# Where tiles lie in the on-chip memory: streamed tiles 64 bytes behind their weights modulo 256, in a two-network fp32 kernel on one Trainium2 core

## The chip, the core and the metric

The kernel runs on one core of a Trainium2 chip. TensorE multiplies, VectorE (DVE) and ScalarE (ACT) do the elementwise work, SyncE (SP) issues the loads, and GpSimd (POOL) has next to nothing to do. The metric is the time on the device in microseconds; a lower one is better. The kernel's median over 3 runs is 2473.17 us (2472.64 to 2473.49).

## The reference

Two networks of two layers each, one after the other, on 256 tokens of 1024 features, all in fp32. Each layer of the first network (block 1) has modulated norms, windowed and grouped-query attention over the tokens and 256 context tokens, two up-projections weighted by gates, and a gated feed-forward. Each layer of the second has a feed-forward, a mixer of three attentions (forgetting, stick-breaking, and one with selected keys), and a second feed-forward. Cut to the products that fill TensorE:

```python
def swiglu_2(h, w_gu, w_down):
    g, u = jnp.split(h @ w_gu, 2, axis=-1)
    return (jax.nn.silu(g) * u) @ w_down

# block 1, per layer
h = modulate(rms_norm(x, norm1[l]), sh1, sc1)
na_q, na_k, na_v, gq, gk, gv, ga, gb = jnp.split(h @ w_in[l], IN_SPLITS, axis=-1)
...
x = x + g1 * branch_merge(ya, yb, ga, gb, w_pa[l], w_pb[l], w_o[l])
h2 = modulate(rms_norm(x, norm2[l]), sh2, sc2)
x = x + g2 * swiglu(h2, w_ffn_in[l], w_ffn_out[l])
# second network, per layer: feed-forward, mixer, feed-forward
(q_a, k_a, v_a, f_a, q_b, ...) = jnp.split(h @ w_in, _split_points(), axis=-1)
```

## The kernel before

Activations are kept transposed: 128 features on the partitions, tokens along the row, and a k-tile is one such block of 128 features. Every fp32 operand of a large product is split into a high and a low half of type float32r. ScalarE writes the high half (`hi`, line 403), VectorE the rest (`lo`, line 408). A product is then three matmuls per weight block: high weights with the high stream, high weights with the low stream, low weights with the high stream (`group`). All are issued on line 427. In the profile's names the streamed tile stands first and the weights second: `mm<-gh,hwf` streams gh against weights hwf. hwb and lwb are weight halves of block 1, hwf and lwf those of the second network's feed-forwards, hwmx and lwmx those of its mixers.

Streams: hh and hl are block 1's inputs (512 columns for tokens and context in layer 0, 256 columns for tokens in layer 1, where keys still need 512); gh and gl the second network's inputs; acth and actl the gated inner activations on their way down; yh, yl, ybh, ybl, mh, ml the outputs of attention and their gated sums. In the value projections the roles are exchanged: the weight tile streams, and hh or gh stands as weights.

Memory comes from pools that are laid out as two stacks, one from the left (low addresses) and one from the right. On the left lie, in this order, the constants `cp`, the weights `wp` (raw tiles, then eight high and eight low tiles of 512 floats), the small tiles `sp`, and then whatever a stage opens. A pool's tiles follow each other, each rounded up to 32 bytes, so that the width of one small tile shifts everything behind it. In the built program the weights' halves begin at 39,552 and 55,936, both 128 modulo 256, and step by 2048. The starts of streams modulo 256 are: gh, gl and block 1's mh, ml 224; acth, actl, ybh, ybl, yh, yl and the mixers' mh, ml 0; block 1's hh and hl first 32 and 160 (layer 0's attention, where yh and yl of its merge lie at 32 too), later 0 and 128. hh and hl have rows of 516 floats per k-tile, 2064 bytes; layer 1's feed-forward uses two columns more than 512 (`unnormed` writes columns 512 and 513). Attention's own tiles lie on the right side, at 224.

The order of instructions is made by a scheduler from the program's own order, with a few ties that the kernel adds. `hold` and `queue` make one of them: after the last instruction of a step, a set number (the skip) of later weight splits on VectorE may pass, and the next ten must wait behind it. MIX_HOLD is the skip for a mixer's last normalised input tile (gl at k-tiles 6 and 7).

Of the kernel before, what the change touches and what calls it, by code (L numbers as in the profile page):

```python
# [8 lines left out]
F32 = mybir.dt.float32  # L9
F32R = mybir.dt.float32r  # L10
# [6 lines left out]
P = 128  # L17
DM = 1024
SEQ = 256
NKT = DM // P  # L20
# [112 lines left out]

MIX_HOLD = 5
MIX_ORDER = (
    "K S0 G8 T0 T1 F0 s0 S2 s1 S1 G1 G9 s3 G10 F1 s2 s4 x0 B3 G5 x2 G4 x1 d1 F2 x3 d0 G2 G0 G11 x4 x5 d2 d3 B1 G7 G3 d4 d5 A0 B2".split()
)
# [177 lines left out]

SWAP1 = [p ^ 1 for p in range(32)]
SWAP2 = [p ^ 8 if p < 16 else p for p in range(32)]

# [44 lines left out]
class Builder:  # L367
# [208 lines left out]
            self.hi(hh[:, k : k + 2, c], t)  # L576
            self.last_norm = self.lo(hl[:, k : k + 2, c], t, hh[:, k : k + 2, c])

    def inputs_of(self, pool):

        return [pool.tile([P, NKT, 516], F32R, tag=f"h{c}", name=self.u(f"h{c}")) for c in "hl"]


    def setup_mod(self):
# [11 lines left out]
    def pad_mod(self, pool):  # L596
        nc = self.nc

        self.scp = pool.tile([P, NKT, 32], F32, name="scp")
        nc.vector.memset(self.scp, 0.0)  # L600
        nc.vector.tensor_copy(self.scp[:, :, :2], self.sc)
        self.four = pool.tile([P, 2], F32, name="four")
        nc.vector.tensor_tensor(self.four, self.ident[:, 0:2], self.ident[:, 32:34], ALU.add)
        for j in (64, 96):
            nc.vector.tensor_tensor(self.four, self.four, self.ident[:, j : j + 2], ALU.add)
# [210 lines left out]
    def block1(self, layers, fill):  # L816
        nc = self.nc
        with self.open("y0") as yp:
            y = self.y_tiles(yp, 2 * SEQ)
            self.pad_mod(yp)  # L820
            w = Weights(self, "wb1_0")
            with self.open("h0") as hp:
                h = self.inputs_of(hp)
                with self.open("n0", "right") as np_:
                    self.xs = []
                    self.mod_first(np_, h)
                with self.open("a0", "right") as self.ap_:
                    gates = self.b1_attention(0, w, *h, y, 2 * SEQ, yp)
            self.xs, self.xstack = [], ExitStack()
            for i, (key, stack) in enumerate((("xT", self.ctx), ("ctxT", self.xstack))):  # L830
                x = stack.enter_context(self.open(key, "right")).tile([P, NKT, SEQ], F32, name=f"x{i}")
                nc.sync.dma_start(x, self.ins[key])
                self.xs.append(x)
            md = ExitStack()
            rest = fill(md.enter_context(self.open("mod", "right")))
            mr = ExitStack()
            m = self.b1_merge(0, w, y[0], gates, mr.enter_context(self.open("mr0", "right")), 2 * SEQ)
        with self.open("hn") as hn:
            for l in range(layers):
                T = SEQ if l else 2 * SEQ  # L840
                if l:
                    with self.open("y1") as yp:
                        y = self.y_tiles(yp, T)
                        w = Weights(self, "wb1_1")
                        with self.open("a1", "right") as self.ap_:
                            gates = self.b1_attention(1, w, *h, y, T, yp)
                        mr = ExitStack()
                        m = self.b1_merge(1, w, y[0], gates, mr.enter_context(self.open("mr1", "right")), T)
                self.tc.keep_in_program_order(nc.scalar.preload_act_table_set("silu_and_others"))
                self.amplitude(l, 1, len(self.xs))  # L850
                h = self.inputs_of(hn)
                self.residual(
                    l, w, range(NKT), m, T, 16, hn, lambda i: self.norm_mod(l, 1, i, self.xs[i], h, hn, self.rsb[i]),
                    early=(lambda k: self.unnormed(l, k, h)) if l else None, place="ac"[l],
                )
                mr.close()
                if l:
                    self.room2()
                with self.open(f"f{l}") as fp:
                    if l == 0 and layers > 1:  # L860
                        h2 = []

                        def norm(i):
                            if not h2:
                                h2.extend(self.inputs_of(hn))
                            self.norm_mod(1, 0, i, self.xs[i], h2, hn, self.rsb[i])

                        self.b1_ffn(0, w, h, fp, hn, T, rest, norm)
                        h = h2
                    else:  # L870
                        self.b1_ffn(l, w, h, fp, hn, T, rest, None)
                if l == 0:
                    md.close()
                    if layers > 1:
                        self.xstack.close()
                        self.xs = self.xs[:1]
                assert w.off == w.ap.shape[0] and w.i == len(w.spec)
# [74 lines left out]
    def b1_attention(self, l, w, hh, hl, y, T, yp):  # L952
# [3 lines left out]
        full = lambda k: (hh[:, k, :512], hl[:, k, :512])  # L956
        mine = lambda k: (hh[:, k, :T], hl[:, k, :T])
        nt = T // P
        qg = self.small(1, tag="qg", bufs=1)
        nc.vector.tensor_scalar(qg, self.p(f"qg{l}"), HD**-0.5, None, ALU.mult)  # L960
        bias_tile = lambda: ap.tile([P, 2, SEQ], F32, tag="bias", name=self.u("bias"), bufs=2)
        rot = bias_tile()
# [77 lines left out]
        n = B1_ORDER[l].index("|")  # L1040
# [302 lines left out]
    def mix_attention(self, l, w, hh, hl, xs, rsb, yh, yl, op, gates):  # L1343
# [23 lines left out]
        for b in (b1, b2):  # L1367
            t = self.t2("rq")
            self.rope(pairs(t), pairs(b), twice(cr), twice(sr), SWAP2)
            q = ap.tile([P, 2, 512], F32R, tag="cq", name=self.u("cq"), bufs=2)  # L1370
# [27 lines left out]
        for k in range(0, NKT, 2):  # L1398
# [6 lines left out]
            last = self.lo(hl[:, k : k + 2], pairs(t), hh[:, k : k + 2])  # L1405
        self.hold(1, last, MIX_HOLD)

# [8 lines left out]
        def keys(_):  # L1416
# [21 lines left out]
            kk = self.t2("kk")[:, :SEQ]  # L1438
            self.rope(ki, ki, cos[:64], sin[:64], SWAP2)
            self.halves(kk, ki)  # L1440
            ik.extend(self.parts("ik", kk, SEQ, bufs=1))
            self.rope(kv[64:, SEQ:], kv[64:, SEQ:], cos[64:], sin[64:], SWAP2)
            qs[0] = ap.tile([P, 2, SEQ], F32R, tag="iq", name=self.u("iq"), bufs=1)
# [106 lines left out]
    def dsa_keys(self, l, kv, cos, sin, vs):  # L1550
# [8 lines left out]
        kc, kk = self.t2("kc")[:64, :SEQ], self.t2("kk")[:, :SEQ]  # L1559
        self.rope(kc, kp[:64, :SEQ], cos[:64], sin[:64], SWAP2)  # L1560
        self.halves(kk, kc)
# [196 lines left out]
            self.rsb = [self.rstd_rows(ss)]  # L1758

    def setup2(self):  # L1760
        self.one = self.cp.tile([P, 1], F32, name="one")
        self.nc.vector.memset(self.one, 1.0)

    def store(self, out):
# [71 lines left out]
```

## Time and profile before

| what | value |
|---|---|
| median of 3 runs | 2473.17 us |
| the profiled execution's own time | 2474.45 us |
| its span, first to last instruction | 2472.6 us |
| mean granted clock of TensorE | 0.988 |
| PE busy | 2404.3 us, 97% |
| DVE busy | 1821.5 us, 74% |
| ACT busy | 1357.2 us, 55% |
| DMA | 159 GB/s mean, q1 48.8% of 16 engines |

The profile is one execution. The difference between its time and its span lies outside the first and the last instruction. A busy matmul is counted to its modelled end; in a back-to-back run the next one starts long before that, so the distance from one start to the next is the time that a matmul costs, and the listed duration of some 280 ns is longer than that distance.

### The profile page before, as it was taken

What the parts mean: (1) busy time and instruction counts of PE and PEld (TensorE: products, weight loads), DVE (VectorE), ACT (ScalarE), POOL (GpSimd) and SP (SyncE); (2) the same over time, 40 slices, a digit from 0 to 9 for tenths busy, and PEclk for the clock granted to TensorE, in tenths of its full rate; (3) what the DMA queues carried; (4) which work ended last, traced back from release to release, by engine and by line L of the source; (5) the groups of instructions that cost most, each with busy time, mean ns of one, the idle gap of its engine ahead of it and who ended that gap; (6) DMA issues with size and microseconds to landing.
All of it is one profiled execution on the core that took longest, in us unless ns stands there. A gap on an engine that the chain in (4) does not pass through costs nothing.

```text
span 2472.6 us, 45747 instructions
## 1 busy us (share of the span) xinstructions
PE 2404.3 (97%) x17232; PEld 2243.4 (91%) x17232; DVE 1821.5 (74%) x4115; ACT 1357.2 (55%) x2666; POOL 0.2 (0%) x4
## 2 busy tenths in 40 slices
PE   7999999999999999999999999999999999999997
PEld 4877779888888898999999998999999999899997
DVE  5777667885766888776676688886666669888665
ACT  4566544322223676665555567765555556776553
POOL 0000000000000000000000000000000000000000
PEclk9999999999999999999999999999999999899999
DMA  7221462553653333465555553455555555345553
GB/s 276 85 73 52 160 232 95 171 188 131 218 184 119 129 112 115 146 187 183 184 182 181 182 183 117 138 173 184 177 186 187 178 184 183 106 135 188 180 179 103
DMA packets 112542, 393.45 MB, mean 159 GB/s; under 512 B 12480, under 2 KB 13760, under 8 KB 111808
## 3 DMA queue, kind: packets, MB, share of 16 engines
q1 hardware_dynamic: 112320, 390.52, 48.8%
q8 instruction: 136, 2.23, 0.4%
q14 instruction: 86, 0.70, 0.1%
HBM read 389.42 MB, written 1.05 MB: 158 GB/s over the span
## 4 chain that ended last, share of the span: by engine, by line
PE 91%; DVE 5%; ACT 2%; issue 1%; DMA 1%; SPq 0%; DVEq 0%; ACTq 0%
PE mm L427 82%; PE y L427 2%; PE s L427 1%; PE s L798 1%; PE mm L616 1%; PE y L805 1%; DVE lwmx L408 1%; PE s L751 1%; PE y L486 0%; DMA wm0r<-in_wm_dram 0%; DVE kl L408 0%; ACT pt L775 0%; ACT hwmx L403 0%; PE y L682 0%; DVE ptl L408 0%
## 5 line engine op out<-in xcount | busy, mean ns | idle before, releaser
L427 PE MATMUL mm<-hh,hwb 128*128 128x512 f32 (+2 forms) x1176 | 349.1, 341 | 3.1 <-ACT gt L1027 1.6
L427 PE MATMUL mm<-hl,hwb 128*128 128x512 f32 (+1 forms) x1176 | 350.0, 340 | 0.2 <-DVE hl L408 0.2
L427 PE MATMUL mm<-hh,lwb 128*128 128x512 f32 (+2 forms) x1176 | 346.7, 340 | 0.0
L403 ACT ACTIVATE hwb<-wb_0r 128x512 fp32r<-128x512 f32 (+1 forms) x250 | 149.9, 612 | 261.4 <-PE mm L427 242.4
L427 PE MATMUL mm<-gh,hwf 128*128 128x256 f32 x1344 | 272.1, 283 | 0.0
L427 PE MATMUL mm<-gh,lwf 128*128 128x256 f32 x1344 | 270.7, 282 | 0.0
L427 PE MATMUL mm<-gl,hwf 128*128 128x256 f32 x1344 | 270.6, 282 | 0.0
L408 DVE TENSOR_TENSOR lwf<-wf_1r,hwf 128x512 fp32r<-128x512 f32 (+1 forms) x272 | 183.8, 676 | 110.2 <-ACT hwf L403 103.9
L408 DVE TENSOR_TENSOR lwf<-wf_0r,hwf 128x512 fp32r<-128x512 f32 (+1 forms) x272 | 183.6, 676 | 103.4 <-ACT hwf L403 96.7
L403 ACT ACTIVATE hwf<-wf_1r 128x512 fp32r<-128x512 f32 (+1 forms) x272 | 168.2, 619 | 166.6 <-PE mm L427 153.7
L403 ACT ACTIVATE hwf<-wf_0r 128x512 fp32r<-128x512 f32 (+1 forms) x272 | 168.2, 619 | 165.3 <-PE mm L427 149.4
L427 PEld LDWEIGHTS mm<-hh,hwb 128*128 128x128 f32 x1176 | 203.7, 189 | 30.3 <-ACT gt L1027 2.7
L408 DVE TENSOR_TENSOR lwb<-wb_0r,hwb 128x512 fp32r<-128x512 f32 (+1 forms) x250 | 163.6, 666 | 89.5 <-ACT hwb L403 85.5
L427 PEld LDWEIGHTS mm<-hl,hwb 128*128 128x128 f32 x1176 | 204.5, 189 | 25.8 <-DVE hl L408 0.8
L427 PEld LDWEIGHTS mm<-hh,lwb 128*128 128x128 f32 x1176 | 203.9, 189 | 25.4
L403 ACT ACTIVATE hwb<-wb_1r 128x512 fp32r<-128x512 f32 (+1 forms) x242 | 146.6, 612 | 117.6 <-PE mm L427 107.3
L427 PEld LDWEIGHTS mm<-gh,hwf 128*128 128x128 f32 x1344 | 207.5, 189 | 0.0
L427 PEld LDWEIGHTS mm<-gh,lwf 128*128 128x128 f32 x1344 | 206.7, 188 | 0.0
L408 DVE TENSOR_TENSOR lwb<-wb_1r,hwb 128x512 fp32r<-128x512 f32 (+1 forms) x242 | 158.5, 667 | 65.2 <-ACT hwb L403 62.5
L427 PEld LDWEIGHTS mm<-gl,hwf 128*128 128x128 f32 x1344 | 205.8, 188 | 0.0
L427 PE MATMUL mm<-gh,hwmx 128*128 128x256 f32 x656 | 140.5, 288 | 4.6 <-DVE kl L408 2.1
L427 PE MATMUL mm<-actl,hwf 128*128 128x256 f32 x704 | 142.0, 283 | 0.0
(393 smaller groups left out, 5558.8 us busy)
## 6 DMA issues: line engine op xcount, KB each, us to landing
wf_0r<-in_wf_dram SPq DMA_DIRECT2D x120, 512.0 KB, 3.5
wf_1r<-in_wf_dram SPq DMA_DIRECT2D x120, 512.0 KB, 3.6
wb_0r<-in_wb_dram SPq DMA_DIRECT2D x108, 512.0 KB, 3.8
wb_1r<-in_wb_dram SPq DMA_DIRECT2D x105, 512.0 KB, 3.7
wmx_0r<-in_wmx_dram SPq DMA_DIRECT2D x49, 512.0 KB, 3.6
wmx_1r<-in_wmx_dram SPq DMA_DIRECT2D x49, 512.0 KB, 3.6
wm2r<-in_wm_dram SPq DMA_DIRECT2D x48, 512.0 KB, 3.6
wm1r<-in_wm_dram SPq DMA_DIRECT2D x24, 512.0 KB, 4.7
```

Of the source, the lines that this page charges most:

```text
L403: self.nc.scalar.activation(out, src, AF.Copy, scale=scale)
L408: return self.nc.vector.tensor_tensor(out, src, h, ALU.subtract)
L427: i = nc.tensor.matmul(out, lhsT, rhs, start=bank not in first, stop=n[bank] == 0, skip_group_check=True)
L616: nc.tensor.matmul(ps[32 * j : 32 * j + 32], self.scp[:, k], t[:, o : o + 512], start=k < 4, stop=k >= 4, skip_group_check=True,)
L751: nc.tensor.matmul(out, q, part, start=n == 0, stop=n == 1, skip_group_check=True)
L798: nc.tensor.matmul(s[:, :nk], q[:, o], part, start=n == 0, stop=n == 1, skip_group_check=True)
L805: nc.tensor.transpose(tp[:, j * P : (j + 1) * P], pt[:, j * P : (j + 1) * P], self.ident)
```

## The change

Five edits shift places, and one changes a tie. `one` grows from 1 column to 9 (36 bytes, so 64 in place of 32), which moves the weights and all behind them by 32 bytes. `qg` becomes a tile of 64 floats in place of 16, which moves what lies behind the small tiles by 192 more. `four` becomes 64 floats in place of 2, another 224 for what lies behind it. `inputs_of` makes rows of 512 floats (2048 bytes per k-tile) in place of 516, and for layer 1's feed-forward rows of 520 (2080 bytes). MIX_HOLD goes from 5 to 6.

In the built program after the change the weights' halves begin at 160 modulo 256, and gh, gl, acth, actl, hh, hl, ybh, ybl, yh, yl, mh, ml all at 224. The value projections stream weights at 160 against hh or gh at 224. Attention's tiles on the right side stay where they were. No matmul is added or taken away.

```diff
@@ -133,7 +133,7 @@
 
 
 
-MIX_HOLD = 5
+MIX_HOLD = 6
 MIX_ORDER = (
     "K S0 G8 T0 T1 F0 s0 S2 s1 S1 G1 G9 s3 G10 F1 s2 s4 x0 B3 G5 x2 G4 x1 d1 F2 x3 d0 G2 G0 G11 x4 x5 d2 d3 B1 G7 G3 d4 d5 A0 B2".split()
 )
@@ -324,6 +324,7 @@
 
 
 
+
 class Weights:
 
 
@@ -576,9 +577,9 @@
             self.hi(hh[:, k : k + 2, c], t)
             self.last_norm = self.lo(hl[:, k : k + 2, c], t, hh[:, k : k + 2, c])
 
-    def inputs_of(self, pool):
-
-        return [pool.tile([P, NKT, 516], F32R, tag=f"h{c}", name=self.u(f"h{c}")) for c in "hl"]
+    def inputs_of(self, pool, n=2 * SEQ):
+
+        return [pool.tile([P, NKT, n], F32R, tag=f"h{c}", name=self.u(f"h{c}")) for c in "hl"]
 
 
     def setup_mod(self):
@@ -599,7 +600,7 @@
         self.scp = pool.tile([P, NKT, 32], F32, name="scp")
         nc.vector.memset(self.scp, 0.0)
         nc.vector.tensor_copy(self.scp[:, :, :2], self.sc)
-        self.four = pool.tile([P, 2], F32, name="four")
+        self.four = pool.tile([P, 64], F32, name="four")[:, :2]
         nc.vector.tensor_tensor(self.four, self.ident[:, 0:2], self.ident[:, 32:34], ALU.add)
         for j in (64, 96):
             nc.vector.tensor_tensor(self.four, self.four, self.ident[:, j : j + 2], ALU.add)
@@ -848,7 +849,7 @@
                         m = self.b1_merge(1, w, y[0], gates, mr.enter_context(self.open("mr1", "right")), T)
                 self.tc.keep_in_program_order(nc.scalar.preload_act_table_set("silu_and_others"))
                 self.amplitude(l, 1, len(self.xs))
-                h = self.inputs_of(hn)
+                h = self.inputs_of(hn, 520 if l else 2 * SEQ)
                 self.residual(
                     l, w, range(NKT), m, T, 16, hn, lambda i: self.norm_mod(l, 1, i, self.xs[i], h, hn, self.rsb[i]),
                     early=(lambda k: self.unnormed(l, k, h)) if l else None, place="ac"[l],
@@ -956,7 +957,7 @@
         full = lambda k: (hh[:, k, :512], hl[:, k, :512])
         mine = lambda k: (hh[:, k, :T], hl[:, k, :T])
         nt = T // P
-        qg = self.small(1, tag="qg", bufs=1)
+        qg = self.sp.tile([P, 64], F32, tag="qg", name=self.u("qg"), bufs=1)[:, :1]
         nc.vector.tensor_scalar(qg, self.p(f"qg{l}"), HD**-0.5, None, ALU.mult)
         bias_tile = lambda: ap.tile([P, 2, SEQ], F32, tag="bias", name=self.u("bias"), bufs=2)
         rot = bias_tile()
@@ -1758,7 +1759,7 @@
             self.rsb = [self.rstd_rows(ss)]
 
     def setup2(self):
-        self.one = self.cp.tile([P, 1], F32, name="one")
+        self.one = self.cp.tile([P, 9], F32, name="one")[:, :1]
         self.nc.vector.memset(self.one, 1.0)
 
     def store(self, out):
```

The built program's order differs in three places: at the end of layer 1's attention in block 1, and in the two mixers. The first place shown is on VectorE in the first mixer, around the last gl (`gl_15786<-hn_16906`). lwmx are low halves of weights, numbered by weight tile and k-tile. Before:

```order
L408 TENSOR_TENSOR lwmx_7_0_17068<-wmx_0r_17065,hwmx_7_0_17067 128x512
L408 TENSOR_TENSOR gl_15786<-hn_16901,gh_15785 128x512
L409 SCALAR_TENSOR_TENSOR vs_16699<-mm_16835,rcol_16417,vs_16699 128x5x64
L409 SCALAR_TENSOR_TENSOR vs_16699<-mm_16836,rcol_16417,vs_16699 128x5x64
L408 TENSOR_TENSOR gl_15786<-hn_16906,gh_15785 128x512
L408 TENSOR_TENSOR lwmx_7_2_17072<-wmx_0r_17065,hwmx_7_2_17071 128x512
```

After, the same stretch:

```order
L409 TENSOR_TENSOR lwmx_7_0_17068<-wmx_0r_17065,hwmx_7_0_17067 128x512
L409 TENSOR_TENSOR gl_15786<-hn_16901,gh_15785 128x512
L409 TENSOR_TENSOR lwmx_7_2_17072<-wmx_0r_17065,hwmx_7_2_17071 128x512
L410 SCALAR_TENSOR_TENSOR vs_16699<-mm_16835,rcol_16417,vs_16699 128x5x64
L410 SCALAR_TENSOR_TENSOR vs_16699<-mm_16836,rcol_16417,vs_16699 128x5x64
L409 TENSOR_TENSOR gl_15786<-hn_16906,gh_15785 128x512
```

One low-half split, lwmx_7_2, now stands ahead of the two value splits (vs) and of that last gl; the others follow as they did.

The second place is on PE at the end of layer 1's attention: the up-projection of yb (streams ybh, ybl into mm_10473), with the transposes of one softmax tile (pt_9880) and the score product of another unit (s_10287) between. Before:

```order
L427 MATMUL mm_10473<-ybl_8116,hwb_1_16_0_10465 128x256 x2
L427 MATMUL mm_10473<-ybh_8115,lwb_1_16_0_10466 128x256 x2
L427 MATMUL mm_10473<-ybh_8115,hwb_1_16_0_10465 128x256
L805 MATMUL y_9892<-const_69,pt_9880 128x128 x4
L427 MATMUL mm_10473<-ybh_8115,hwb_1_16_0_10465 128x256
L427 MATMUL mm_10473<-ybl_8116,hwb_1_16_0_10465 128x256 x2
L427 MATMUL mm_10473<-ybh_8115,lwb_1_16_0_10466 128x256 x2
L427 MATMUL mm_10473<-ybh_8115,hwb_1_16_2_10469 128x256 x2
L427 MATMUL mm_10473<-ybl_8116,hwb_1_16_2_10469 128x256 x2
L427 MATMUL mm_10473<-ybh_8115,lwb_1_16_2_10470 128x256 x2
L427 MATMUL mm_10473<-ybh_8115,hwb_1_16_2_10469 128x256 x2
L427 MATMUL mm_10473<-ybl_8116,hwb_1_16_2_10469 128x256 x2
```

After:

```order
L428 MATMUL mm_10473<-ybl_8116,hwb_1_16_0_10465 128x256 x2
L806 MATMUL y_9892<-const_69,pt_9880 128x128 x4
L428 MATMUL mm_10473<-ybh_8115,lwb_1_16_0_10466 128x256 x2
L428 MATMUL mm_10473<-ybh_8115,hwb_1_16_0_10465 128x256 x2
L428 MATMUL mm_10473<-ybl_8116,hwb_1_16_0_10465 128x256 x2
L428 MATMUL mm_10473<-ybh_8115,lwb_1_16_0_10466 128x256 x2
L428 MATMUL mm_10473<-ybh_8115,hwb_1_16_2_10469 128x256 x2
L799 MATMUL s_10287<-k_10071,q_10066 128x512
L799 MATMUL s_10287<-kl_10072,q_10066 128x512
L428 MATMUL mm_10473<-ybl_8116,hwb_1_16_2_10469 128x256 x2
L428 MATMUL mm_10473<-ybh_8115,lwb_1_16_2_10470 128x256 x2
L428 MATMUL mm_10473<-ybh_8115,hwb_1_16_2_10469 128x256 x2
```

The four transposes stand three matmuls earlier, and the two score matmuls come into this stretch, 16 matmuls of the products earlier than before. On SP the loads of two weight tiles that follow (wb_1) stand one or two rows later; ScalarE's and VectorE's rows of the same stretch shift with the work that they feed.

## Rows read from the trace of the kernel before

**Rows 1.** The page: span, and each engine's busy time, share and instructions.

```profile
span 2472.6 us, 45747 instructions
...
PE 2404.3 (97%) x17232; PEld 2243.4 (91%) x17232; DVE 1821.5 (74%) x4115; ACT 1357.2 (55%) x2666; POOL 0.2 (0%) x4
```

**Rows 2.** The page: the chain that ended last, by engine and by line.

```profile
PE 91%; DVE 5%; ACT 2%; issue 1%; DMA 1%; SPq 0%; DVEq 0%; ACTq 0%
PE mm L427 82%; PE y L427 2%; PE s L427 1%; PE s L798 1%; PE mm L616 1%; PE y L805 1%; DVE lwmx L408 1%; PE s L751 1%; PE y L486 0%; DMA wm0r<-in_wm_dram 0%; DVE kl L408 0%; ACT pt L775 0%; ACT hwmx L403 0%; PE y L682 0%; DVE ptl L408 0%
```

**Rows 3.** Windows: stretch, length, busy us (count) of PE, PEld, DVE, ACT, POOL, clock, DMA.

```profile
1490.00:1640.00 150.00, 142.87 (x1148) 140.12 (x1147) 130.77 (x364) 108.21 (x254) 0.00 (x0) 0.97 0.41 130
1640.00:1840.00 200.00, 200.00 (x1678) 200.00 (x1677) 138.36 (x258) 113.21 (x199) 0.00 (x0) 1.00 0.59 184
```

**Rows 4.** Windows of PE alone: stretch, length, busy us (count), clock, DMA share, GB/s.

```profile
1680.00:1770.00 90.00, 90.00 (x753) 1.00 0.60 186
1880.00:1970.00 90.00, 90.00 (x752) 1.00 0.59 183
1800.00:1840.00 40.00, 40.00 (x340) 1.00 0.59 184
1990.00:2030.00 40.00, 40.00 (x340) 1.00 0.57 181
1075.00:1165.00 90.00, 90.00 (x766) 1.00 0.63 188
...
701.60:716.24 14.64, 14.64 (x64) 1.00 0.71 236
```

**Rows 5.** Timeline of PE: start, us until the last end, instruction, count merged.

```profile
1090.18 0.41 PE L427 MATMUL mm<-hh,hwb 128*128 128x256 f32 x2
...
1091.84 0.39 PE L427 MATMUL mm<-hl,hwb 128*128 128x256 f32 x2
1092.07 0.40 PE L427 MATMUL mm<-hh,lwb 128*128 128x256 f32 x2
...
1093.25 0.40 PE L427 MATMUL mm<-hl,hwb 128*128 128x256 f32 x2
1093.49 0.40 PE L427 MATMUL mm<-hh,lwb 128*128 128x256 f32 x2
...
1095.84 0.41 PE L427 MATMUL mm<-hh,hwb 128*128 128x256 f32 x2
```

**Rows 6.** Tile hl in four short windows: ns minimum, median, maximum; first, last start.

```profile
L427 PE MATMUL mm<-hl,hwb x1: 392/392/392, 708.8 to 708.8; 128*128 128x512 f32 x1
...
L427 PE MATMUL mm<-hl,hwb x1: 400/400/400, 710.2 to 710.2; 128*128 128x512 f32 x1
...
L427 PE MATMUL mm<-hl,hwb x2: 277/278/279, 1091.8 to 1092.0; 128*128 128x256 f32 x2
...
L427 PE MATMUL mm<-hl,hwb x2: 280/282/284, 1093.3 to 1093.4; 128*128 128x256 f32 x2
```

**Rows 7.** Groups by shape: line, engine, operation, tiles, count | busy us, mean ns.

```profile
L427 PE MATMUL mm<-gh,hwf 128*128 128x256 f32 x1344 | 272.1, 283 | 0.0
...
L427 PE MATMUL mm<-hh,hwb 128*128 128x512 f32 x592 | 228.9, 398 | 1.6 <-ACT hh L403 0.9 <-ACT gt L1027 0.7
...
L427 PE MATMUL mm<-acth,hwf 128*128 128x256 f32 x704 | 141.0, 282 | 0.0
...
L427 PE MATMUL mm<-gh,hwmx 128*128 128x256 f32 x656 | 140.5, 288 | 4.6 <-DVE kl L408 2.1 <-ACT fw L1395 1.7 <-DVE gate L1548 0.8
...
L427 PE MATMUL mm<-hl,hwb 128*128 128x256 f32 x584 | 124.3, 284 | 0.0
```

**Rows 8.** PE's waits in 975 to 1025, 1430 to 1490 and 1490 to 1640 us.

```profile
PE mm L427 <- ACT gt L1027: 1.1, 1, 1.1
...
PE mm L427 <- ACT fw L1395: 0.8, 1, 0.8
...
PE s L1689 <- ACT ph L403: 3.1, 2, 2.6
```

## Prediction

> **What bounds the kernel now.** I read the page first: TensorE's matmuls are busy for 2404.3 of a span of 2472.6 us [rows 1], and the chain of waits runs through PE for 91% of the span, 82% of it line 427, where the products of the weights are issued [rows 2]. The other engines are not near their limit: over the 200 us of a feed-forward block of the second network VectorE is busy for 138 us and ScalarE for 113 us, and PE for all 200 [rows 3]. So time goes where TensorE's back-to-back matmuls go, and the question is how long one of them takes.
>
> The table of windows answers that, since in dense stretches a window's length over its count of matmuls is the distance from start to start. A window also counts the records that are still running when it opens, two of 256 columns or one of 512, which I take off. Gate and up products (tiles gh, gl): 90 us over 751 and over 750, 119.9 ns each. Down products (tiles acth, actl): 40 us over 338, twice, 118.3 ns. Layer 1 of block 1 (hh, hl): 90 us over 764, 117.8 ns [rows 4]. All three are 128x128 weights against 256 columns, at a granted clock of 1.00, the 2.4 GHz level, with PE never idle; they differ by 2 ns, and in nothing that the instruction's shape shows.
>
> What they differ in is where the streamed tile lies. The weights' high and low halves all begin at byte 128 modulo 256. gh and gl begin at 224, a distance of 96 behind their weights; acth and actl at 0, a distance of 128; hh and hl have rows of 516 floats, 2064 bytes, so that each k-tile lies 16 bytes further modulo 256 and the distance runs through 128, 144, ... 240 for hh and 0, 16, ... 112 for hl. That third stretch thus holds the price of every distance. It repeats itself exactly: 24 pairs of matmuls from 1090.18 to 1095.84 us, 48 in 5.66 us, 117.9 ns each. In it the pair of hl at k-tile 4, distance 64, takes from 1091.84 to 1092.07, and the pair at k-tile 6, distance 96, from 1093.25 to 1093.49 [rows 5]: 0.23 against 0.24 us. The durations, which stand in whole ns, say the same: 278 ns in the median at distance 64, 282 at 96; and with 512 columns 392 at 64 against 400 at 96 [rows 6].
>
> **The price per distance.** At 64 I take 115.5 ns per matmul of 256 columns: half of 0.23 us is 115, and I leave half a ns for the rounding. At 96 half of 0.24 is 120, and the long uniform run at 96 measured 119.9, so that here a price read from single pairs held in a uniform run as well; that is my reason to carry the 115.5 over to uniform runs at 64, which the trace doesn't have. The bounds: 114.5 if every matmul became as short as the shortest in the pair (277 against 278), and 119.9, the dearest uniform run, on the other side. For 512 columns the run from 701.60 to 716.24 has 63 matmuls in 14.64 us, 232.4 ns [rows 4]. The 392 at distance 64 lies 5 ns under the 397 or so of the whole group [rows 7], the 400 at 96 lies 3 above it. These are single records, so at 64 I take 230.3, a little under half of the 5 ns; bounds 227.4 and 235.4.
>
> **The change part by part.** *Distance 96 to 64.* Weights move to 160, gh and gl stay at 224. By the groups, with the two sister groups that repeat each row: three times 1344 against wf, three times 656 against wmx, three times 64 in the spare bank, three times 160 of block 1's merge, 6,672 matmuls [rows 7]. 6,672 x (119.9 - 115.5) = 29.4 us.
>
> *Distance 128 to 64.* acth, actl, yh, yl, ybh, ybl and the mixers' mh, ml move from 0 to 224: 3 x (704 + 260 + 144 + 128 + 32 + 32) = 3,900, of which the largest group has its row [rows 7]. 3,900 x (118.3 - 115.5) = 10.9 us.
>
> *Block 1's inputs.* With rows of 512 floats the k-tiles no longer drift. The products of 512 columns number 3 x (592 + 134 + 64 + 16) = 2,418 [rows 7]; 2,418 x 2.1 = 5.1 us. Those of 256 columns number 584 + 560 + 560 = 1,704; of these the 936 of layer 1's feed-forward (19 weight tiles of 48, and 24 of the first three) keep a drift, now of 32 bytes per k-tile (rows of 520 floats), and I leave them at 117.8, with 1 ns either way as bounds; 768 x (117.8 - 115.5) = 1.8 us.
>
> *What streams the weights.* The value projections stream weight tiles against hh or gh as weights, 576 matmuls that go to a distance of 192. No uniform row has it; I cost it at nothing, 1.5 ns either way, 0.9 us. Attention's own tiles, in pools on the right side, keep their places.
>
> *The order.* MIX_HOLD puts one more low-half split (0.6 us on VectorE) ahead of the last gl in each mixer, and the scheduler shifts score products and transposes by a few matmuls in the mixers and at the end of layer 1's attention; SP gets two weight loads one row later. PE's waits that this could touch are 1.1 us for gt at layer 1's end, 0.8 us for fw at a mixer's start, and 3.1 us for ph in the middle of one [rows 8], the last two again in the second mixer. I cost it at nothing; if all these waits went it would be 9 us less, and as much more if each doubled. The cover of the moved split is thin, with VectorE busy for 131 of 150 us in a mixer [rows 3]; if it is gone, the last gl comes 0.6 us later, once per mixer.
>
> *Sum.* 29.4 + 10.9 + 5.1 + 1.8 = 47 us. Part of that lies in attention and mixers, where the chain leaves PE: a stretch of 150 us in a mixer has 7 us of PE idle [rows 3], and a chain of softmax steps doesn't shorten when the products between them do. I take off an eighth, 6 us: 41 us. The profiled execution took 2474.45 us, 1.28 above the median of the runs; 2474.45 - 41 = 2433.4, and against the median 2432.
>
> The Trainium skill, page "TensorE: Matmul & The Clock Gate", section "Back-to-back issue gap", gives N / 2.4 + 2.5 ns, 109 ns for 256 columns as an estimate from that page. The rows above show 118 to 120, so this kernel has some 10 ns per matmul that the rule doesn't know; by the rule there would be nothing for a place to give back.
>
> **The rivals.** *The distance is an accident of the stage.* Gate/up, down and block 1 have different evictions beside them, and the 2 ns could be theirs. For it: no uniform run at 64 exists. Against it: within one stretch, with the same evictions, pairs of 0.23 and 0.24 us recur with the k-tile. Then nothing but the order changes: 2473, from 2469 to 2477. The Trainium skill, page "SBUF — State Buffer", section "SBUF: two separate sides", speaks for this rival: only the port shared by VectorE and GpSimd contends, and TensorE has two independent read ports. By that rule the time would stay at 2473; the pairs at 64 and 96 disagree with it.
>
> *The tile's own place sets the price.* In all these rows the weights lie at 128, so distance and place are one number. hl at distance 64 lies at 192 and at distance 96 at 224. After the change nearly all streams lie at 224, the place of gh and gl, the dearest. Then the 6,672 stay at 119.9, the 3,900 lose 1.6 ns each (6.2 us), the 768 lose 2.1 (1.6 us), the 2,418 of 512 columns lose 3 (7.3 us): 15 us slower, 2488. It decides from the first gate/up run on. Against it stand the value projections, whose streams always lie at 128 and whose weights drift, but they have no uniform row to settle it.
>
> *Waits take the gain.* TensorE runs dry more often since the splits come at their old pace. In the dense stretches VectorE and ScalarE have 30% and 43% to spare [rows 3], so this can hold in mixers and attention alone: a gain of half, 2453. Its mark is that PE's idle time grows by some 20 us.
>
> **How the numbers follow.** My forecast 0.72, waits take half 0.07, accident of the stage 0.08, own place 0.13. A difference under 0.2% (5 us) can't be told from none. Faster: 0.72 + 0.07 = 0.79; same 0.08; slower 0.13. The likeliest case by itself runs from 2408 (114.5 and 227.4 ns throughout, nothing taken off: 36 + 15 + 12 + 2 = 65 us) to 2450 (half of the 47 us). For eight times in ten I let in the case of no change at the upper end, 2474, and 3 us of moved waits at the lower, 2405.
>
> **What would show it.** Right: in a gate/up window of 90 us some 781 matmuls in place of 753, in a down window of 40 us 348 in place of 340, the 512-column run at 230 ns, while layer 1's gate/up of block 1 stays at 766 within 8; PE's idle time up by no more than 6 us. If gate/up stays at 753 and down falls to 336, the own place was it; if all counts stay, the stage. The forecast is wrong as a whole if a uniform run at 64 is not under 118 ns.

## The result, and the profile after

The changed kernel takes 2444.54 us in the median of its runs (2444.41 to 2447.11), against 2472.9 of the kernel before on the same chip: a ratio of 0.9888, with an interval of 0.9871 to 0.9905. That is 28 us less; 41 were forecast. The execution that was profiled took 2447.11 us, and its span is 27.3 us shorter than before's.

The page of the changed kernel has the span, the busy times, and the chain of waits by engine and by line:

```profile
span 2445.3 us, 45747 instructions
...
PE 2374.1 (97%) x17232; PEld 2219.9 (91%) x17232; DVE 1819.9 (74%) x4115; ACT 1356.8 (55%) x2666; POOL 0.2 (0%) x4
...
PE 90%; DVE 5%; ACT 2%; DMA 1%; issue 1%; SPq 0%; DVEq 0%; ACTq 0%
```

Against [rows 1, 2], PE's busy time fell by 30.2 us and its idle time (span less busy) rose from 68.3 to 71.2. So the time came out of the matmuls themselves: the same 17,232 of them, with the same shapes.

The windows of PE in the changed kernel, in the stages of [rows 4] (gate and up twice, down twice, block 1's second feed-forward); the columns are as there:

```profile
1660.00:1750.00 90.00, 90.00 (x767) 1.00 0.61 186
1860.00:1950.00 90.00, 90.00 (x766) 1.00 0.59 185
1780.00:1820.00 40.00, 40.00 (x342) 1.00 0.58 189
1965.00:2005.00 40.00, 40.00 (x343) 1.00 0.64 190
1070.00:1160.00 90.00, 90.00 (x766) 1.00 0.61 186
```

With the two running records taken off, gate and up went from 119.9 to 117.7 ns a matmul and down from 118.3 to 117.5. A window's count is coarse; by the starts themselves, without the first gaps of a run, both now take 117.8 ns (120.0 and 118.7 before), so they have one price. The gate and up windows hold 767 and 766 matmuls, where the forecast looked for 781, and the down windows 342 and 343 against 348. Block 1's second feed-forward, which still drifts, did not change. The groups by shape that answer to [rows 7]:

```profile
L428 PE MATMUL mm<-gh,hwf 128*128 128x256 f32 x1344 | 267.3, 280 | 0.0
L428 PE MATMUL mm<-hh,hwb 128*128 128x512 f32 x592 | 228.8, 398 | 1.7 <-ACT hh L404 0.8 <-ACT gt L1028 0.7 <-DVE kl L409 0.2
L428 PE MATMUL mm<-acth,hwf 128*128 128x256 f32 x704 | 139.9, 279 | 0.0
L428 PE MATMUL mm<-gh,hwmx 128*128 128x256 f32 x656 | 137.2, 284 | 2.4 <-DVE kl L409 1.9 <-ACT fw L1396 0.5
L428 PE MATMUL mm<-hl,hwb 128*128 128x256 f32 x584 | 124.1, 283 | 0.0
```

The duration of the 512-column group is no shorter (398 ns), though its start-to-start is. In the longest unbroken run of 512 columns (244 gaps; its first few gaps are left out here and below) the mean gap is 232.4 ns before and 228.9 after. Durations overlap; a run's price is the distance between starts. A window of that run in the changed kernel, cut like the last line of [rows 4], has 63 matmuls in 14.42 us in place of 14.64:

```profile
533.23:547.65 14.42, 14.42 (x64) 1.00 0.48 161
```

### The profile page after: what moved, and what is told of

Its sections match the earlier page's. It is cut to its first block, busy times and chain, and to the rows that moved or that the text cites. A ratio compares the mean times of both kernels' runs of the same rounds, so it can differ in the third digit from the quotient of the medians.

```text
span 2445.3 us, 45747 instructions
## 1 busy us (share of the span) xinstructions
PE 2374.1 (97%) x17232; PEld 2219.9 (91%) x17232; DVE 1819.9 (74%) x4115; ACT 1356.8 (55%) x2666; POOL 0.2 (0%) x4
## 4 chain that ended last, share of the span: by engine, by line
PE 90%; DVE 5%; ACT 2%; DMA 1%; issue 1%; SPq 0%; DVEq 0%; ACTq 0%
PE mm L428 81%; PE y L428 2%; PE s L428 1%; PE s L799 1%; PE y L806 1%; DMA wm0r<-in_wm_dram 1%; PE mm L617 1%; DVE lwmx L409 1%; PE s L752 1%; DVE kl L409 1%; PE y L487 0%; DMA wb_0r<-in_wb_dram 0%; ACT hwmx L404 0%; PE y L683 0%; ACT pt L776 0%
## 5 line engine op out<-in xcount | busy, mean ns | idle before, releaser
L428 PE MATMUL mm<-acth,hwf 128*128 128x256 f32 x704 | 139.9, 279 | 0.0
```

The lines of the kernel that those rows point to most:

```text
L428: i = nc.tensor.matmul(out, lhsT, rhs, start=bank not in first, stop=n[bank] == 0, skip_group_check=True)
```

## The experiments

Three theories went in. A: the distance from weights to stream modulo 256 sets a matmul's price. B: the stream's own place sets it. C: the order (MIX_HOLD) took or gave part of the time.

**Distance 96 and 128, by moving the weights alone.** `one` lies ahead of the weights and `qg` behind them, ahead of all streams. Floats taken from one and given to the other move the weights and the small tiles between the two. Streams stay at 224.

```
d96:   -one = tile([P, 9])   +one = tile([P, 1])     -qg = tile([P, 64])   +qg = tile([P, 72])
d128:  -one = tile([P, 9])   +one = tile([P, 57])    -qg = tile([P, 64])   +qg = tile([P, 16])
```

> The changed kernel with the weights 32 bytes lower (128 modulo 256) and every stream left at 224, so that all distances of 64 become 96; PE's order is the same. Theory A, the distance of a stream behind its weights sets the price: gate and up return from 117.7 to 119.9 ns per matmul, down goes from 117.6 to 119.9 as well, the 512-column products from 229 to about 235; 11,460 x 2.3 + 2,418 x 5.6 = 40 us, so about 2480, slower than the kernel before. Theory B, the stream's own place sets it: all streams stay at 224, so 2444 within 5. Theory C, the gain came from the scheduler's order and MIX_HOLD: 2444 as well.

> The changed kernel with weights 64 bytes lower (96 modulo 256), streams at 224: distance 128 everywhere. Theory A: uniform runs at 118.3 ns as down had before, so 11,460 x 0.7 = 8 us, and 512 columns at about 232, 2,418 x 3 = 7 us: about 2459. Theories B and C: 2444 within 5. The price per distance as read from pairs in a drifting run (119.2 at 128 against 115.5 at 64) would make it 2485; that reading already failed for 64.

Measured: 2479.86 us at 96 (ratio 1.0028, 1.0017 to 1.0039) and 2465.54 at 128 (0.9969, 0.9957 to 0.998). The weights' move by 32 bytes took back the whole gain and 7 us more. Theory A had 2480 at 96, and its figure for 128 was some 6 us too low.

**Same distance, all places 32 bytes lower.**

```
both32:  -one = tile([P, 9])   +one = tile([P, 1])
         +a tile [P, 8] at the start of the right side
```

> The changed kernel with weights, streams and attention's tiles all 32 bytes lower: weights at 128, streams at 192, distance 64 as in the changed kernel. Theory A: 2444.5 within 3, uniform runs at 117.7. Theory B: place 192 is the one that had the short pairs (115.5) in the kernel before, so about 2420.

Measured: 2444.23 us (0.9885, 0.9868 to 0.9902). Streams at 192 in place of 224 made no difference, so B falls. This run settles a further rival, the own place of the weights: d96 and both32 have their weights and small tiles at the same places, 128 modulo 256 for the weights, and differ by 36 us.

**The order.** `hold5` is the changed kernel with the old MIX_HOLD, `hold6` the kernel before with the new one.

```
hold5 (on after):   -MIX_HOLD = 6   +MIX_HOLD = 5
hold6 (on before):  -MIX_HOLD = 5   +MIX_HOLD = 6
```

> The changed kernel with MIX_HOLD back at 5, places untouched. Theory A: the order is worth nothing within 3 us, 2442 to 2448. Theory C: the order carries a good part of the 28 us, so over 2455.

> The kernel before with MIX_HOLD = 6 and nothing else. Theory A (as forecast, the order is worth nothing on the old places): 2470 to 2476 us, mixers at 229 us each. Theory C (MIX_HOLD = 6 is a better order whatever the places, worth the 17 us that 5 cost on the new ones): 2455 to 2460, mixers at 221. Theory D (the mixers' table fits one of the two values by accident of the places): between 2470 and 2495.

Measured: hold6 took 2472.29 us (0.9997, 0.9987 to 1.0006), no change, as the forecast had it. But hold5 took 2461.7 us (0.9953, 0.9938 to 0.9968), 17 us slower than the changed kernel, which A had put at no change: a miss. On the old places the table's value moves 58 of the matmuls in the trace; on the new places it moves some 1,100. The new places alone had already changed the order: hold5 and the kernel before have the same table value, and some 1,400 matmuls stand differently. With 5 that order is a bad one. The waits of PE in 1585 to 1612 us, in the first mixer, first hold5 (columns: us, times, longest):

```profile
PE y L428 <- ACT ph L404: 2.4, 3, 1.0
PE s L752 <- ACT pt L776: 0.7, 1, 0.7
PE mm L428 <- DVE yl L409: 0.3, 1, 0.3
```

and the changed kernel in the same stretch:

```profile
PE s L752 <- ACT pt L776: 0.8, 1, 0.8
PE mm L428 <- DVE gate L1549: 0.2, 1, 0.2
```

PE's windows in both mixers, first hold5 (the number behind the count is the granted clock):

```profile
1590.00:1610.00 20.00, 16.71 (x114) 0.91 0.20 66
2110.00:2140.00 30.00, 25.10 (x166) 0.77 0.24 79
2200.00:2215.00 15.00, 12.22 (x69) 0.77 0.19 58
```

then the changed kernel:

```profile
1590.00:1610.00 20.00, 18.94 (x158) 1.00 0.40 128
2110.00:2140.00 30.00, 25.43 (x169) 0.77 0.21 68
2200.00:2215.00 15.00, 14.75 (x126) 1.00 0.53 155
```

The timeline of PE in hold5 there (start, us until the last end, instruction; in brackets the idle time before it and its releaser):

```profile
1594.23 0.39 PE L428 MATMUL y<-ph,vs 128*128 128x256 f32 x1 [0.58 <-ACT ph L404]
...
1596.79 0.39 PE L428 MATMUL y<-ph,vs 128*128 128x256 f32 x1 [0.81 <-ACT ph L404]
...
1599.29 0.38 PE L428 MATMUL y<-ph,vs 128*128 128x256 f32 x1 [0.98 <-ACT ph L404]
```

and its windows there and right after:

```profile
1590.00:1600.00 10.00, 6.80 (x44) 0.98 0.26 79
1600.00:1610.00 10.00, 9.91 (x71) 0.85 0.15 54
```

In hold5 three attention products within 6 us each wait for their ph, with little between them: PE is busy for 6.80 of 10 us, and the clock is lower right after. PE's idle time is 79.3 us by its page (2459.4 less 2380.1), 8.1 more than in the changed kernel. In the first and third window the granted clock falls below the 2.4 GHz level, which it doesn't in the changed kernel: 9% of 20 us and 23% of 15 us, 1.8 + 3.4 us. Idle time and clock together make 13.3 of the 14.1 us between the two spans. In the middle window the clock falls in both alike. That waits set the clock off is the order of events in the trace; no run took the waits alone away. Why other places make the scheduler choose another order was not tried.

**The whole circle of distances.** The same two edits give the rest; all have the order of the changed kernel.

```
        one    qg             one    qg             one    qg
d0      25     48      d160   49     24      d224   33     40
d32     17     56      d192   41     32
```

> The streams' places move to the weights' own place modulo 256 (distance 0 in place of 64 nearly everywhere; block 1's drifting products shift by the same 64 bytes and keep their mean). The order of instructions is that of the changed kernel. Theory A (the distance modulo 256 sets a matmul's price): the change's time plus about 1.5 ns for each of some 10,000 matmuls at uniform distance, by the pairs of the drifting run of before at distance 0 (11.8 ns above the columns' own time, against 12.1 at 128 and 9.7 at 64), so near 128's 2465 us: 2457 to 2470. Theory B (only 64 is cheap because of something else in the layout, and any other move by less than a bank costs nothing): 2444. Theory C (the price is a step function of overlap, highest when both start at one place): over 2480.

> Distance 32 nearly everywhere, order of instructions as in the changed kernel. Theory A by the pairs of before (11.3 ns at 32, 12.1 at 128, 9.7 at 64): between 64 and 128, 2452 to 2465 us. Rival: 64 and 32 belong to one cheap stretch: 2442 to 2447. Rival: a distance that is not a multiple of 64 is dear as such (96 was): near 2480.

> Distance 160 nearly everywhere, order of instructions as in the changed kernel. By the runs at 128, 192 and 224 (2465.5, 2431.7, 2463.2): the price falls from a ridge to a dip at 64 and at 192, so 160 lies like 224, which is as far from 192: 2455 to 2466. By symmetry about 128 (96 gave 2479.9): 2475 to 2483. By repetition after 128 bytes (32 gave 2446.7): 2444 to 2450.

> Distance 192 nearly everywhere, order of instructions as in the changed kernel. Theory A with the price taken from pairs of the changed kernel's own drifting run (8.0 ns at 192, the cheapest there): faster than the change, 2420 to 2440 us. Theory A with the pairs of before (11.9 ns at 192): 2457 to 2468. If neither kind of pair carries over to a run at one distance, anything between 2440 and 2480.

> Distance 224 nearly everywhere, order of instructions as in the changed kernel. Theory A by the pairs of before (11.4 ns at 224): 2453 to 2465 us. Rival, that a distance not a multiple of 64 is dear as such (96 was): near 2480.

Measured, with the mean from start to start in uniform runs of 256 columns (gate and up) and in the longest run of 512; two values stand where long runs of one kernel went at two prices:

```
distance      256 cols, ns       512 cols, ns   median us   ratio (95%)
0             120.0              226.7          2464.97     0.9969 (0.9957 to 0.998)
32            116.7              233.3          2446.71     0.9893 (0.9878 to 0.9908)
64 (after)    117.8 (113.3)      228.9          2444.54     0.9888 (0.9871 to 0.9905)
96            120.0              233.3          2479.86     1.0028 (1.0017 to 1.0039)
128           118.7              233.3          2465.54     0.9969 (0.9957 to 0.998)
160           117.3 or 118.7     234.3          2460.93     0.9956 (0.9941 to 0.9971)
192           117.8 or 113.3     233.3          2431.71     0.9834 (0.9819 to 0.9848)
224           118.3              233.3          2463.16     0.996  (0.9945 to 0.9974)
```

A window of the longest 512-column run and the first gate and up window after the first mixer. At 0:

```profile
532.00:582.00 50.00, 50.00 (x222) 1.00 0.42 137
1690.00:1740.00 50.00, 50.00 (x419) 1.00 0.59 182
```

At 96:

```profile
532.00:582.00 50.00, 50.00 (x220) 1.00 0.42 137
1690.00:1740.00 50.00, 50.00 (x419) 1.00 0.60 181
```

The gate and up window alone, at 32:

```profile
1690.00:1740.00 50.00, 50.00 (x431) 1.00 0.64 189
```

At 128:

```profile
1690.00:1740.00 50.00, 50.00 (x424) 1.00 0.58 186
```

So the price does hang on the distance, and 64 is not its best value. The prices also account for the times, to 2 us at four distances and to some 4 at 32: 11,460 matmuls of 256 columns and 2,418 of 512 went from 64 to the distance of each run, and their two differences of price give 20 us more than the changed kernel at 0, 36 at 96, 21 at 128, 17 at 224 and 2 less at 32, where 20.4, 35.3, 21.0, 18.6 and 2.2 more were measured (160 and 192 go at two prices, and are left out). Two rivals fall by the same runs. One is that VectorE's and ScalarE's work beside the products sets the price: in the longest gate and up run at 0, 938 of 940 gaps are 120 ns, while VectorE is busy for 75 and ScalarE for 64 of 112 us. The other is a circle longer than 256: in the built programs the streams of gate and up lie 256 bytes further from their weights modulo 512 than those of down, and at 0, 64 and 96 both have one price. What in the chip makes the price hang on the distance no run shows.

The expectations built on single pairs of a drifting run hit at 0 and at 224, and missed at 32, where the 256-column price is lower than the pairs said; 160 was forecast from the runs beside it, and hit. The hit at 0 is luck: it rests on 11.8 ns over the columns' own time, where the longest drifting run of before has 9.1 to 9.4. At 192 the pairs of before said 2457 to 2468 and the pairs of the changed kernel 2420 to 2440: two drifting runs gave two prices for one distance, and the second happened to be right. The two column counts don't rank the distances alike either: 0 is, with 96, the dearest for 256 columns and the cheapest for 512.

**Two rhythms at one distance.** At 192 a run of 256 columns goes at 117.8 or at 113.3 ns, and in these traces stays at one until something else comes between; at 160 the two are 118.7 and 117.3. Two gate and up windows of the kernel at 192:

```profile
1690.00:1740.00 50.00, 50.00 (x427) 1.00 0.61 188
1880.00:1930.00 50.00, 50.00 (x443) 1.00 0.64 193
```

The timeline of its PE where the down products change from one to the other (start, us until the last end, instruction, count merged):

```profile
1783.74 0.40 PE L428 MATMUL mm<-acth,lwf 128*128 128x256 f32 x2
1783.98 0.40 PE L428 MATMUL mm<-acth,hwf 128*128 128x256 f32 x2
1784.21 0.40 PE L428 MATMUL mm<-actl,hwf 128*128 128x256 f32 x2
...
1784.93 0.38 PE L487 MATMUL y<-const,sq 128*128 128x128 f32 x2
1785.06 0.48 PE L428 MATMUL mm<-actl,hwf 128*128 128x256 f32 x2
...
1785.85 0.39 PE L428 MATMUL mm<-actl,hwf 128*128 128x256 f32 x2
1786.08 0.39 PE L428 MATMUL mm<-acth,lwf 128*128 128x256 f32 x2
```

Two short matmuls of the norm (128 columns) come between. Before them the gaps from start to start are 117 to 119 ns (the last one 123), and from the sixth gap after them on 113 and 114, with the same tiles and no wait on either side. At 64 the fast rhythm is rare in the changed kernel; in both32 and in rows576 it also takes most of 1260 to 1360 us.

**Block 1's last drift taken away.**

```
rows576:  -h = self.inputs_of(hn, 520 if l else 2 * SEQ)   +h = self.inputs_of(hn, 576 if l else 2 * SEQ)
```

> The changed kernel with block 1's second inputs 2304 bytes a k-tile in place of 2080, so that they too stand at distance 64 throughout; order unchanged. By the uniform price at 64 (117.8 ns) against the drifting mean (117.8 ns in the same stretch): no difference, 2442 to 2447 us. By the forecast's price (115.5): 3 us faster, 2440 to 2442. If the 113.3 ns rhythm takes the stretch: 2438 to 2441.

Measured: 2440.78 us (0.9871, 0.9857 to 0.9886). PE's windows of rows576, first a stretch of gate and up further on, then the stretch that was changed:

```profile
1270.00:1350.00 80.00, 80.00 (x708) 1.00 0.59 195
1070.00:1160.00 90.00, 90.00 (x766) 1.00 0.59 186
```

The stretch whose places changed has the 766 of the changed kernel. The first has 708 where the changed kernel has 681: the fast rhythm, some 706 x 4.5 ns = 3.2 of the 3.8 us that were gained, in instructions and places that the edit didn't touch. So the gain isn't the edit's: the uniform price at 64 and the drifting mean are the same.

**The best of both.** Distance 192 for block 1's second feed-forward and all of the second network ("blocks 2 to 5" below), and 0 for nearly all that streams 512 columns in block 1, with the 256-column products beside it ("block 0" is block 1's first layer).

```
mix (on d192):  -four = tile([P, 64])   +four = tile([P, 16])
                +a tile [P, 16] first in pool hn;  +a tile [P, 48] first in pool f1
                -h = self.inputs_of(hn, 520 ...)   +h = inputs_of(hn, 576 ...)[:, :, 48:] in layer 1
```

> The kernel with distance 192, with block 0's inputs (and what streams behind them, with 512 and with 256 columns) at distance 0 and block 1's second inputs with k-tiles 2304 bytes apart, so at 192 throughout; the order of the matmuls is unchanged. Theory A (distance sets the price, another one for 512 columns than for 256): the 512-column stretches take 110.3 us for 500 matmuls as at distance 0 and not 113.3 as at 192, some 9 us less in all, and block 1's second feed-forward 0 to 5 us less: 2417 to 2424 us. Rival (block 0's 192-column and 0-column stretches differ because of the right-hand tiles, which don't move here): 2430 to 2433. On the two rhythms seen at 192 (113.3 and 117.8 ns for a matmul): if a start's phase picks them, the same instructions at the same places in blocks 2 to 5 show them in other stretches than before, and the total moves by up to 10 us to either side; if the place alone picks them, in the same stretches.

Measured: 2414.16 us (2409.12 to 2422.06), ratio 0.9768 (0.9748 to 0.9789): 59 us under the kernel before, 30 under the changed one. It went below the expected range. The 512-column run is at 226.7 ns, as at distance 0. Its windows of PE, two of gate and up as above, then block 1's second feed-forward:

```profile
1690.00:1740.00 50.00, 50.00 (x443) 1.00 0.64 190
1880.00:1930.00 50.00, 50.00 (x427) 1.00 0.58 183
...
1070.00:1160.00 90.00, 90.00 (x796) 1.00 0.62 193
```

In the third the fast rhythm has the whole stretch (796 against 766), and over all long gate and up runs the mean is 114.5 ns where d192 has 115.7: some 4 us each, by 911 and 3,849 gaps. The range had counted the first; the second is what lies below it. In the first two the rhythms are swapped against d192, though neither the order nor any place differs in those blocks. So the place alone doesn't pick the rhythm. The switch behind two short matmuls points at how a run starts, but that is argued and not shown: no run set the start of a run by itself.

## Why the prediction was right, and where its sizes were off

*The distance is the cause: right.* It held against own place (both32 for the streams, both32 with d96 for the weights) and against an accident of the stage (d96, d128: other times with the same order of instructions). The runs at eight distances span 48 us. The rule that the forecast set beside the first rival, from the Trainium skill (page "SBUF — State Buffer", section "SBUF: two separate sides"), would have left all eight at one time; the measurements decide against it.

*The price of 115.5 ns at 64: this step failed in size.* The forecast took it from pairs in a drifting run and carried it to uniform runs because at 96 the same step had held; that agreement was luck. The uniform run at 64 takes 117.7 by the windows (117.8 by the starts), just under the 118 that was set as the mark for being wrong as a whole. With measured prices the terms are:

- distance 96 to 64: 6,672 x (119.9 - 117.7) = 14.7 us, not 29.4
- distance 128 to 64: 3,900 x (118.3 - 117.5) = 3.1 us, not 10.9
- 512 columns: 2,418 x (232.4 - 228.9) = 8.5 us, not 5.1
- block 1's other 768: 768 x (117.8 - 117.7) = 0.1 us, not 1.8

That is 26.4 us, and the spans differ by 27.3. So nothing was left over for the eighth (6 us) that the forecast took off for attention and mixers; without that allowance the forecast would have been 47 and not 41, further away. That this allowance and the 512-column term, too low by 3 us, offset part of the price's error is luck too, and the time lies in the range since the range let in half of the sum and no change at all.

Why the pairs misled: in a drifting run a gap belongs to its neighbours too. Over the 38 matmuls at distance 64 in the longest drifting run of the kernel before, the gap to the next start has a mean of 115.6 ns and the gap from the start before 118.8; which of the two is called its price decides whether 64 is cheap. At distance 0 the two are 116.1 and 115.8 in the same run, and 120.0 in a uniform one. The uniform prices of the eight distances have a mean of 118.4 ns (with 117.8 at 192 and 118.0 at 160), near the drifting run's 117.8, so the sum of a drift is about right, but its split over the distances is not. One agreement, at 96, was no proof for 64.

*The order at nothing: right between these two kernels, by luck.* Alone the new MIX_HOLD is worth nothing (hold6). Without it the new places would have brought 11 us and not 28 (hold5). The bound of 9 us for PE's waits was too narrow for that case, since it left out the clock.

*Waits take the gain: did not happen.* PE's idle time rose by 2.9 us, under the 6 that were allowed. *Block 1's second feed-forward stays at 766:* it did. *The 512-column run at 230:* 228.9.

## What to carry to other kernels

Where TensorE is busy all the time, look at the gap from start to start in a uniform run and ask whether it differs between stages of one shape: here the places of operands alone moved the time by 48 us, and the best mixture of them lies 59 under the kernel before. Read such a price only from a run that is uniform, or try all the distances, since single pairs in a mixed run carry their neighbours' share. And after a change of places retune the order: a table value that is worth nothing on one layout was worth 17 us on the next.

## What the runs showed of the hardware that was not expected

- A 128x128 by 256-column matmul with its weight load takes from 113.3 to 120.0 ns from start to start at the full clock, by the distance of stream to weights. At 2.4 GHz 113.3, 116.7 and 120.0 ns are 272, 280 and 288 cycles: 16, 24 and 32 more than there are columns. 512 columns take 226.7 ns at distance 0, 228.9 at 64, and 233.3 to 234.3 elsewhere in the longest run (at 128 two shorter runs took 232.3).
- At 64, 160 and 192 two stable rhythms exist. In the trace of d192 they change behind two short matmuls. The executions of mix ran from 2409 to 2422 us; the rhythm of the others isn't in a trace, so that it is the cause of the spread is likely and not shown.
- In hold5 three waits of 0.58 to 0.98 us within 6 us were followed by a granted clock of 0.85 in the next 10 us, so that the loss in clock came on top of the waits.
